# One expert's halves instead of two experts' quarters: how the second layer's expert weights are cut into transfers

## The chip, the cores and the metric

The kernel runs on one core of one Trainium2 chip. Its metric is the device time of one execution in microseconds (us); the median of three runs is used. A profile is one execution seen by the hardware profiler: which instruction ran when on which engine, what it waited for, and what the core's 16 transfer (DMA) engines moved.

## The reference

Two small networks run one after the other over 256 tokens of width 1024 (272 with the meta tokens of the first one). The part that matters is the mixture of experts in the first network, which comes twice, once per layer. Each token is sent to two of 32 experts, and each expert is three matrices:

```
def expert_block(args):
    xb, e = args
    hb = jax.nn.silu(xb @ w_gate[e]) * (xb @ w_up[e])
    return hb @ w_down[e]
```

`w_gate[e]` and `w_up[e]` are 1024 x 512, `w_down[e]` is 512 x 1024, all in 32-bit floats: 2 MB each, 6 MB an expert, 192 MB a layer. All 32 experts are read in both layers, since nearly every one has some tokens. Behind the second layer's experts come a layer norm and the second network (a state-space mixer, an MLP, attention, an MLP).

## The kernel before, in words

**Quads.** `moe(layer, ...)` works on four experts at a time, a quad; `qd` runs from 0 to 7, and its experts begin at `e0 = 4 * qd`. Each expert has 32 places for tokens. Four experts' 32 columns stand side by side on TensorE, so each matmul of line 983 (gate and up, 32 columns of stationary operand, 512 of moving weights) runs beside those of three other experts. A quad has 64 such products, which the trace shows as 128 matmul records (two for each), and 32 down products of line 1035, 64 records. Between them stand silu and the product hh (lines 1002 and 1003), four transposes of hh (line 1008), two of the token placement (1016) and a small gate product (1019). After the down products come eight records of line 1047, which carry the result back to the tokens. For every second quad, `gather` (line 935) brings the tokens of the next eight experts to their places.

**Weights.** `load(e)` fetches the 24 MB of a quad in 24 transfers of 1 MB, all issued on SP's queue by `fetch` (line 458), in program order. Each goes to the next buffer of a ring. There are two ways of cutting:

- `half(w, hf)`: one expert's half matrix a transfer, four transfers for the quad; every partition gets one run of 8 KB.
- `quarter(w, kq)`: a quarter matrix of two experts a transfer, two transfers for the quad; every partition gets two runs of 4 KB.

Gate and up products walk the pieces in the order in which they were fetched. With halves, 16 products (32 records) use four buffers, and the loop over the four experts is the innermost one; with quarters, 8 products (16 records) use two. A down half serves 16 products (32 records), a down quarter 8 (16 records). The choice is made on lines 910 to 916:

```
fine = layer == 1 and e >= FINE
if fine:
    gu = [[quarter(I[nm], kq) for nm in ("moe_w_gate", "moe_w_up")] for kq in range(4)]
else:
    gu = [[half(I[nm], hf) for nm in ("moe_w_gate", "moe_w_up")] for hf in range(2)]
if e < 28:
    return gu, [quarter(I["moe_w_down"], j) for j in range(4)] if fine else [half(I["moe_w_down"], hf) for hf in range(2)]
```

With FINE = 8, quads 0 and 1 of the second layer come in halves, as all of the first layer does; quads 2 to 7 come in quarters. The last quad's down matrices (e = 28) are cut by columns, in both kernels alike (lines 918 to 922).

**Buffers.** The ring has 17 buffers of 1 MB when the second layer's experts begin. The generator `stages()` is advanced at seven places in each quad (lines 986, 1005, 1027, 1056, 1060); after 14 steps, within quad 2 and after its loads have been placed, it gives up all but six buffers and adds two (`self.shrink(); self.grow(2)`). So quads 3 to 7 have eight. The space goes to `s5_prepare`, the preparation of the state-space mixer, which the following steps of the same generator put between the experts' instructions (lines 1258 to 1504): DVE computes small tables (W on lines 1405 to 1409, CL on 1424 to 1428), and TensorE turns them (lines 1371, 1373, 1415, 1437, 1458). A transfer into a buffer waits on SP until the matmuls that read the buffer's previous contents are done; all later transfers stand behind it on that queue.

**Order.** Each engine works through its instructions in one fixed order, which is set when the program is built; independent instructions of later steps can be put ahead of waiting ones in it. This is how gathers and the preparation come to stand between gate, up and down products.

Of the kernel before, what the change touches and what calls it, by code (L numbers as in the profile page):

```python
# [40 lines left out]
KV = 1  # L41
WARMB = 3
G3 = 5
FINE = 8
EARLY = 1, 0
N0 = 3
FAST = (0, 1), (0, 1)
# [26 lines left out]
class Net:  # L74
# [709 lines left out]
    def moe(self, layer, rows, stages=()):  # L784
# [10 lines left out]
        with ExitStack() as ph:  # L795
# [94 lines left out]
            def load(e):  # L890
# [18 lines left out]

                fine = layer == 1 and e >= FINE  # L910
                if fine:
# [1152 lines left out]
```

## Time and profile before

| what | value |
|---|---|
| runs | 1826.03, 1827.01, 1830.57 us; median 1827.01 us |
| profiled execution: its time, its span | 1828.64 us, 1826.8 us |
| TensorE (PE) busy | 1555.8 us (85%) |
| VectorE (DVE) busy | 851.4 us (47%) |
| ScalarE (ACT) busy | 504.8 us (28%) |
| SP's transfer queue | 532.04 MB, 76.9% of 16 engines' span |
| experts, first layer | from 142 us (first gate product) to 595 us (last down product) |
| experts, second layer | from 719 us to 1197 us, likewise |

The span runs from the first to the last instruction; the execution's own time is 1.8 us more. Busy shares are averages over stages with different limits. In the experts' stages the transfer engines are nearly always busy, and what the queue moves in a GB/s figure is the measure of progress; in the stages behind them TensorE is. A row of the timeline merges neighbouring instructions of one line, and what stands in square brackets is the idle time before it and what ended that.

### The profile page before, as it was taken

Reading aid. Unit: us, or ns where it says so; the run is one execution under the profiler, and the core shown is the slowest. Engines: PE = TensorE matmul, PEld = TensorE weight load, DVE = VectorE, ACT = ScalarE, POOL = GpSimd, SP = SyncE. Lnnn points to the kernel's source line nnn. Section 1 sums busy time; section 2 is a strip of 40 time slices with the busy share of each in tenths; the row PEclk is TensorE's granted clock in tenths of the full one; section 3 lists DMA queues with packets and bytes.
Section 4 is the critical chain, followed back from the end, with each engine's and each line's share of the span. In section 5 each row is a group of like instructions: output and inputs, shape, how many; then the busy total and the mean of one; then the engine's idle time right before and its main releaser. Section 6 shows DMA issues by size and latency. Waiting matters only on the chain.

```text
span 1826.8 us, 24952 instructions
## 1 busy us (share of the span) xinstructions
PE 1555.8 (85%) x10068; PEld 1022.4 (56%) x10076; DVE 851.4 (47%) x1812; ACT 504.8 (28%) x813; POOL 122.4 (7%) x185
## 2 busy tenths in 40 slices
PE   7898777877886899787696797678999999999997
PEld 6773322311322897232152252157989998889997
DVE  5962111201311874111552265069676556975655
ACT  4721000100000542110110110034454444655441
POOL 3000000000100321000000010012100000100100
PEclk9988989988999999998898898899999999999999
DMA  9449999999999866999999999994745542445520
GB/s 303 158 185 380 420 420 420 420 419 420 410 420 390 322 239 234 420 415 401 395 388 407 368 376 409 389 210 166 251 141 183 190 148 101 162 154 183 187 100 24
DMA packets 150522, 535.59 MB, mean 293 GB/s; under 512 B 23141, under 2 KB 35686, under 8 KB 120698
## 3 DMA queue, kind: packets, MB, share of 16 engines
q1 hardware_dynamic: 148226, 532.04, 76.9%
q0 software_dynamic: 1856, 1.75, 0.4%
q8 instruction: 82, 1.34, 0.3%
q14 instruction: 46, 0.38, 0.1%
q10 hardware_dynamic: 312, 0.07, 0.0%
HBM read 526.49 MB, written 1.05 MB: 289 GB/s over the span
## 4 chain that ended last, share of the span: by engine, by line
PE 36%; DMA 14%; DVE 7%; ACT 2%; issue 1%; SPq 1%; POOL 1%; DVEq 0%; ACTq 0%; POOLq 0%
DMA raw<-in_moe_w_up 7%; PE mm L502 5%; PE mm L504 5%; PE mm L503 5%; DMA raw<-in_moe_w_down 4%; PE tp L503 3%; PE tp L502 3%; PE tp L504 3%; PE mm L983 3%; DMA raw<-in_moe_w_gate 3%; PE mm L1035 2%; PE tp L935 1%; PE tp L1458 1%; SPq L96 1%; DVE raw L1575 1%
## 5 line engine op out<-in xcount | busy, mean ns | idle before, releaser
L983 PE MATMUL mm<-raw,xg 128*32 128x512 f32 x2048 | 371.9, 690 | 144.3 <-DMA raw<-in_moe_w_up 86.7
L295 DVE TENSOR_TENSOR wlo<-raw,whi 128x1024 fp32r<-128x1024 f32 (+3 forms) x265 | 280.3, 1073 | 162.6 <-ACT whi L294 161.8
L983 PEld LDWEIGHTS mm<-raw,xg 128*32 128x32 f32 x2048 | 82.2, 121 | 408.0 <-DMA raw<-in_moe_w_up 151.4
L294 ACT CAST whi<-raw 128x1024 fp32r<-128x1024 f32 (+3 forms) x265 | 238.9, 920 | 243.8 <-PE mm L504 101.5
L1003 DVE TENSOR_TENSOR hh<-hh,mm 128x512 f32<-128x512 f32 x16 | 11.0, 688 | 416.0 <-PE mm L983 391.3
L1035 PE MATMUL mm<-raw,ht 128*32 128x512 f32 (+2 forms) x1120 | 191.5, 593 | 13.8 <-DMA raw<-in_moe_w_down 13.2
L502 PE MATMUL mm<-whi,f 128*128 128x512 f32 (+3 forms) x432 | 149.9, 347 | 0.0
L503 PE MATMUL mm<-wlo,f 128*128 128x512 f32 (+3 forms) x432 | 149.8, 347 | 0.0
L504 PE MATMUL mm<-whi,f 128*128 128x512 f32 (+3 forms) x432 | 149.2, 345 | 0.2 <-DVE f L419 0.2
L503 PE MATMUL tp<-f,whi 128*128 128x256 f32 x512 | 146.0, 285 | 2.6 <-DVE f L419 2.5
L502 PE MATMUL tp<-f,whi 128*128 128x256 f32 x512 | 145.5, 285 | 0.4 <-ACT f L413 0.4
L504 PE MATMUL tp<-f,wlo 128*128 128x256 f32 x512 | 145.6, 284 | 0.0
L1035 PEld LDWEIGHTS mm<-raw,ht 128*32 128x32 f32 x1120 | 48.1, 114 | 119.5 <-issue 83.4
L1002 ACT ACTIVATE hh<-mm 128x512 f32<-128x512 f32 x16 | 9.6, 597 | 359.2 <-PE mm L983 359.2
L503 PEld LDWEIGHTS tp<-f,whi 128*128 128x128 f32 x512 | 99.0, 193 | 3.2 <-DVE f L419 3.2
L502 PEld LDWEIGHTS tp<-f,whi 128*128 128x128 f32 x512 | 98.7, 193 | 1.3 <-ACT f L413 0.9
L504 PEld LDWEIGHTS tp<-f,wlo 128*128 128x128 f32 x512 | 99.1, 194 | 0.0
L503 PE MATMUL mm<-xl,whi 128*128 128x272 f32 (+2 forms) x320 | 93.1, 292 | 0.7 <-DVE xl L295 0.4
L502 PE MATMUL mm<-xh,whi 128*128 128x272 f32 (+2 forms) x320 | 92.3, 292 | 0.9 <-ACT xh L422 0.5
L504 PE MATMUL mm<-xh,wlo 128*128 128x272 f32 (+2 forms) x320 | 91.7, 289 | 0.0
L502 PEld LDWEIGHTS mm<-whi,f 128*128 128x128 f32 x432 | 81.8, 189 | 10.3
L504 PEld LDWEIGHTS mm<-whi,f 128*128 128x128 f32 x432 | 81.5, 189 | 10.4 <-DVE f L419 0.5
(617 smaller groups left out, 2378.2 us busy)
## 6 DMA issues: line engine op xcount, KB each, us to landing
raw<-in_moe_w_gate SPq DMA_DIRECT2D x128, 1024.0 KB, 14.3
raw<-in_moe_w_up SPq DMA_DIRECT2D x128, 1024.0 KB, 19.9
raw<-in_moe_w_down SPq DMA_DIRECT2D x120, 1024.0 KB, 18.0
raw<-in_w_ff SPq DMA_DIRECT2D x64, 1024.0 KB, 5.1
raw<-in_sc_w_in SPq DMA_DIRECT2D x12, 1024.0 KB, 12.4
raw<-in_lru_w_in SPq DMA_DIRECT2D x8, 1024.0 KB, 13.7
raw<-in_ssm_w_glu SPq DMA_DIRECT2D x8, 1024.0 KB, 10.5
raw<-in_moe_w_down SPq DMA_DIRECT2D x12, 512.0 KB, 13.3
```

Of the source, the lines that this page charges most:

```text
L96: return lambda *a, **k: self.tc.keep_in_program_order(f(*a, **k))
L294: f(self.nc.scalar.copy)(hi, src)
L295: f(self.nc.vector.tensor_tensor)(lo, src, hi.bitcast(F32), op=OP.subtract)
L502: mm(out, lhsT=lh, rhs=rh, start=first, stop=False, skip_group_check=shared)
L503: mm(out, lhsT=lh, rhs=rl, start=False, stop=False, skip_group_check=shared)
L504: mm(out, lhsT=ll, rhs=rh, start=False, stop=last, skip_group_check=shared)
L935: nc.tensor.matmul(o, lhsT=hk[n][:, k, :], rhs=P[n], start=n == 0, stop=n == 1)
L983: nc.tensor.matmul(gu[m][i * 32:(i + 1) * 32, :], lhsT=xg[hf][:, k, c], rhs=wgu[hf * n + part][m][i][:, k % (4 // n), :], start=hf == 0 an ...
L1003: v.tensor_tensor(hh, hh, gu[1], op=OP.mult)
L1035: nc.tensor.matmul(o[e * 32:(e + 1) * 32, :], lhsT=ht[:, j, e * 32:(e + 1) * 32], rhs=w[e], start=j == 0, stop=j == 3)
L1458: nc.tensor.matmul(po[:, e, j:4, :], lhsT=sel[:, 67 - 64 * g - j:195 - 64 * g - j], rhs=t[:, g, :, 0:4 - j, :], start=e == slice(0, 8) and ...
L1575: v.tensor_tensor(o[:, :, 1:64], m2[:, :, 0:63], t[:, :, 0:63], op=OP.mult)
```

## The change

One constant: the first expert of the second layer whose quad comes in quarters. With 32 there is none, so `half` serves all quads of both layers, apart from the last quad's down matrices, which stay cut by columns.

```
@@ -41,7 +41,7 @@
 KV = 1
 WARMB = 3
 G3 = 5
-FINE = 8
+FINE = 32
 EARLY = 1, 0
 N0 = 3
 FAST = (0, 1), (0, 1)
```

The order in which the queue fetches a quad changes with it: gate and up alternate in groups of four transfers instead of two, and the down matrices come as two groups of four instead of four groups of two. The number of transfers, their size, and the number of matmuls stay the same.

## Rows read from the trace of the kernel before

**Rows 1.** Windows: stretch, length, busy PE, PEld, DVE, ACT, POOL, PEclk, DMA share, GB/s.
```profile
200.00:260.00 60.00, 47.43 (x244) 18.96 (x236) 10.27 (x22) 4.82 (x8) 0.00 (x0) 0.96 1.01 420
...
900.00:920.00 20.00, 13.58 (x94) 4.82 (x96) 2.40 (x8) 2.26 (x4) 0.00 (x0) 1.00 1.02 409
940.00:960.00 20.00, 20.00 (x144) 11.75 (x144) 7.67 (x12) 3.46 (x5) 0.00 (x0) 1.00 0.98 376
...
1005.00:1025.00 20.00, 17.75 (x108) 6.86 (x108) 8.67 (x16) 4.07 (x7) 0.00 (x0) 0.89 0.86 315
1080.00:1100.00 20.00, 20.00 (x145) 10.82 (x139) 16.19 (x40) 2.76 (x4) 5.75 (x6) 1.00 0.92 335
...
866.00:1168.00 302.00, 232.03 (x1450) 99.68 (x1449) 131.00 (x318) 33.81 (x55) 10.37 (x16) 0.90 1.00 392
```

**Rows 2.** Waits, 850 (DVE: 866) to 1170: us in total, times, longest.
```profile
SPq L458 <- PE mm L983: 113.1, 53, 8.9
SPq L458 <- PE mm L1035: 92.2, 24, 11.2
...
PE tp L1415 <- DVE W L1409: 14.7, 3, 6.9
...
PE mm L1035 <- DMA raw<-in_moe_w_down: 0.6, 1, 0.6
...
DVE hh L1003 <- PE mm L983: 61.9, 3, 25.4
```

**Rows 3.** The page, DMA packets of the whole span by size.
```profile
DMA packets 150522, 535.59 MB, mean 293 GB/s; under 512 B 23141, under 2 KB 35686, under 8 KB 120698
```

**Rows 4.** Timeline of TensorE, quad 3 into quad 4: start us, length us, what.
```profile
911.13 1.91 PE L983 MATMUL mm<-raw,xg 128*32 128x512 f32 x12 [1.51 <-DMA raw<-in_moe_w_up]
913.90 0.75 PE L1008 MATMUL tp<-ident,hh 128*128 128x128 f32 x4 [0.86 <-DVE hh L1003]
...
928.87 1.94 PE L1035 MATMUL mm<-raw,ht 128*32 128x512 f32 x16
...
942.54 1.91 PE L1035 MATMUL mm<-raw,ht 128*32 128x512 f32 x8
...
955.50 6.95 PE L983 MATMUL mm<-raw,xg 128*32 128x512 f32 x57
```

**Rows 5.** Timeline of TensorE, quad 4 into quad 5.
```profile
979.94 0.74 PE L1008 MATMUL tp<-ident,hh 128*128 128x128 f32 x4 [0.86 <-DVE hh L1003]
...
994.88 3.63 PE L1035 MATMUL mm<-raw,ht 128*32 128x512 f32 x24
...
1011.96 1.91 PE L1035 MATMUL mm<-raw,ht 128*32 128x512 f32 x8
...
1016.46 7.07 PE L983 MATMUL mm<-raw,xg 128*32 128x512 f32 x64
```

**Rows 6.** Timeline of TensorE, quad 6 into quad 7.
```profile
1117.98 1.13 PE L1008 MATMUL tp<-ident,hh 128*128 128x128 f32 x4 [6.23 <-DVE hh L1003]
...
1128.65 1.91 PE L1035 MATMUL mm<-raw,ht 128*32 128x512 f32 x8 [0.60 <-DMA raw<-in_moe_w_down]
...
1138.89 4.06 PE L983 MATMUL mm<-raw,xg 128*32 128x512 f32 x16 [1.42 <-DMA raw<-in_moe_w_up]
```

**Rows 7.** Timelines of SP and TensorE: a gate quarter's issue, and its first matmul.
```profile
1018.41 1.16 SPq L458 DMA_DIRECT2D raw<-in_moe_w_gate  x2
...
1023.71 1.05 PE L983 MATMUL mm<-raw,xg 128*32 128x512 f32 x4 [0.17 <-DMA raw<-in_moe_w_gate]
```

**Rows 8.** Timeline of TensorE, quad 5 into quad 6.
```profile
1044.40 0.74 PE L1008 MATMUL tp<-ident,hh 128*128 128x128 f32 x4 [0.86 <-DVE hh L1003]
...
1048.57 6.67 PE L1035 MATMUL mm<-raw,ht 128*32 128x512 f32 x32
...
1071.29 1.91 PE L1035 MATMUL mm<-raw,ht 128*32 128x512 f32 x8
...
1086.70 1.91 PE L983 MATMUL mm<-raw,xg 128*32 128x512 f32 x12
```

More of the change, by code (lines that the diff above doesn't have):

```diff
@@ L43 @@
 G3 = 5
-FINE = 8
+FINE = 32
 EARLY = 1, 0
```

## Prediction, made before the changed kernel was built or run

> **What bounds the kernel now.** I read the page first, then the stage of the second layer's experts by windows, then what the transfer queue and the engines wait for there, and last TensorE's order of work at the four places where one quad (four experts) hands over to the next.
>
> The windows give the two rates of a full transfer queue [rows 1]. With 8 KB runs (first layer, 200 to 260 us) it moves 420 GB/s, so a MB takes 1.048576/0.420 = 2.50 us. With 4 KB runs (900 to 920 us) it moves 409 GB/s, 2.56 us. Quads 3 to 7 of the second layer, 866 to 1168 us, average 392 GB/s: the bytes moved at 409 would take 302 x 392/409 = 289.5 us, so 12.5 us are lost. Three windows hold most of that: 376, 315 and 335 GB/s in 20 us each lose 1.6 + 4.6 + 3.6 = 9.8 us. The other 2.7 us are spread out, and I leave them as they are.
>
> The waits say whose those gaps are [rows 2]. The queue waits 113.1 us for the gate and up matmuls (L983) and 92.2 us for the down matmuls (L1035) to give a buffer back. Most is harmless, because megabytes issued earlier are still moving; the three slow windows are where they ran out. Down matmuls wait 0.6 us for data in the whole stretch: their weights are there long before TensorE comes to them. So the stage is bound by transfers as long as TensorE gives buffers back in time, and at the end of a quad it is late.
>
> **The change, part by part.** Quads 2 to 7 keep 24 transfers of 1 MB each; no instruction is added or dropped on TensorE, and SP issues as many. What moves is (1) the run length, (2) the order of bytes, and (3) how many buffers one stretch of matmuls holds.
>
> (1) Runs. 136 MB (quads 2 to 6, and gate and up of quad 7) go from 4 to 8 KB runs: 136 x (2.564 - 2.497) = 9.1 us less when the queue is full, of which quad 2 has 24 x 0.067 = 1.6. That long runs reach the engines uncut can be counted: the page has 150,522 - 120,698 = 29,824 packets of 8 KB [rows 3], and the 232 MB that already come in halves make 232 x 128 = 29,696. The Trainium skill ("DMA: Bandwidth & Descriptors", section on why small descriptors are slow) charges about 3 cycles a packet beside one per 32 bytes: 131 cycles for 4 KB against 129.5 a half of 8 KB, 1.2%. By that rule the gain is an estimated 4 us, and the sum below would end 5 us higher; the rows show 2.7%, and I take the rows.
>
> (2) and (3) Buffers. From quad 3 on there are eight. A quarter's 16 matmuls hold two and give them back together; six remain ahead. A half's 32 matmuls go through four experts in the inner loop, so all four buffers come back only with the last 8 of the 32. The groups of a quad are now gate-1, up-1, gate-2, up-2, down-1, down-2, four MB each, and each goes into the buffers of the group but one before it. So next quad's gate-1 waits for down-1 to be read, its up-1 for down-2, its gate-2 for its own gate-1.
>
> Call T the arrival of up-2's last MB, S the start of the four transposes of hh (L1008). Now S comes 2.8 us after T (911.13, 913.90) [rows 4]. With halves 26 matmuls instead of 12 are left at T. A row of 64 takes 7.07 us, 0.11 each [rows 5], so 14 more cost 1.5 us: S = T + 4.3, rounded to 4.5 because some stretches run slower (16 take 4.06 us at 1138.89 [rows 6]). On a queue that has run dry, issue to use takes 5.3 us (issue 1018.41, matmul 1023.71) [rows 7]. On a full queue down-2 ends at T + 20 and the next MB at T + 22.5. Let a, b and c be the times from S to the end of the 32nd down matmul, the 64th, and next quad's 32nd gate matmul. Then the queue stands idle, where the value is above zero,
> - ahead of gate-1 for a + 4.5 + 5.3 - 22.5 = a - 12.7,
> - ahead of up-1 for b - g - 10, with g the larger of a and 12.7 (four MB take 10 us),
> - ahead of gate-2 for c - u - 10, with u the larger of b and g + 10.
>
> I take a, b and c from before's rows, since there TensorE works through these stretches with next to no wait for data:
> - Quad 3 [rows 4]: S 913.90; the 32nd is the eighth of the 16 at 928.87, about 929.9; the 64th ends 944.45; the 32nd gate matmul is the ninth of the 57 at 955.50, about 957. a = 16.0, b = 30.6, c = 43.1. Idle 3.3 + 4.6 + 2.5 = 10.4 us.
> - Quad 4 [rows 5]: S 979.94; the eighth of 24 at 994.88, about 996; 1013.87; half of the 64 at 1016.46, about 1020.1. a = 16.0, b = 33.9, c = 40.2. Idle 3.3 + 7.9 + 0 = 11.2 us.
> - Quad 5 [rows 8]: S 1044.40; 1055.24; 1073.20; 1088.61. a = 10.8, b = 28.8, c = 44.2. Idle 0 + 6.1 + 5.4 = 11.5 us.
> - Quad 6 [rows 6]: S 1117.98, b = 1130.56 - 1117.98 = 12.6, c under 25. No idle.
>
> Together 33.1 us. a and b are this long because the program puts the state-space preparation and the next quads' gathers between the down matmuls: 64 of these alone take some 13 us (32 in 6.67 [rows 8]). A wait inside gate and up can cost too: TensorE waits for DVE's W three times, 14.7 us in all, 6.9 at most [rows 2]; the one in quad 3 falls into up-1's reading and now delays up-2. Reading a group takes 3.5 us and a restart 5.3 - 2.5 = 2.8, which leaves 3.7 of the 10 us of the next group, so this costs between 0 and 3 us; I take 1, as part of the wait falls where TensorE has no weights yet. SP stays behind a waiting issue for the same time as the idle sum; only weights are queued there, and nobody else waits on SP in this stage.
>
> Sum for quads 3 to 7: bytes at the long-run rate 302 x 392/420 = 281.9, spread loss 2.7, idle 34.1: 318.7 us against 302, **+16.7**. Quad 2, on the seventeen buffers, -1.6. The last quad's down columns keep their form and follow up-2 as before: 0. After the experts every phase starts from their result, so the rest only shifts. +15.1 on the profiled execution's 1828.6 is 1843.7; that execution is 1.6 over the median, so **1842**.
>
> Bounds. The waits for DVE inside b and c might not move along: if W is ready at the same absolute time, most of its 14.7 us drop out of them; with 11 gone, +4 is left: 1831. If TensorE works at the slower spacing of [rows 6] at each up-2, 3 us more in four quads, or if W comes later too (below), +12 to +15: 1857.
>
> **Rivals.**
> - *Only the rate counts, faster.* The order on TensorE is made when the program is built, and other waits may draw the side work out of the down stretches into gate and up, where TensorE idles. Should a stay under 12.7, b under 22.7 and c under 32.7 in each quad, no new gap opens, and 281.9 + 12.5 = 294.4 us: with quad 2, -9.2, 1818. For it: quad 6 already looks so. Against: three of four quads don't, and the side work has to go somewhere; TensorE is busy for 232 of the 302 us [rows 1]. The Trainium skill ("Trainium Kernel Development and Optimization", best practices) says to double-buffer so that transfers overlap with compute. Four buffers read while four fill is just that, and by that rule alone this rival would hold. The trace speaks against it: with groups of two, and so six MB ahead instead of four, the queue already falls to 315 GB/s.
> - *The two cancel.* If the waits for W stay where they are and half of the side work moves, idle is about 20 us instead of 34: 1828, within the measurement.
> - *DVE is late too, slower still.* hh on DVE waits 61.9 us for gate and up [rows 2], and DVE works in order: what it prepares for TensorE stands behind hh. As hh comes later in each quad, W does too, and the 14.7 us double: 1857. Against it: DVE is busy 131 of 302 us [rows 1] and can catch up.
> - *It doesn't do what it says*: runs might be cut anyway. The packet count [rows 3] excludes this for the first layer's form, which is the same code.
>
> **How the numbers follow.** A measurement tells about 0.3%, 5.5 us, from no change. The forecast's case, starving by fours, has 0.66; DVE late too 0.14; cancelling 0.08; the rate alone 0.12. So faster 0.12, same 0.08, slower 0.80. The range from 1826 to 1862 leaves out the rate alone and the far end of the case in which DVE is late too.
>
> **What would show it.** Right: windows without idle at 420 GB/s, between 870 and 1190 us gaps of 3 to 8 us at three of the quad boundaries, issues of gate-1 right after the 32nd down matmul, and the stage of experts about 15 us longer with everything after it shifted alike. More packets of 8 KB by 136 x 128 = 17,408. Wrong: a mean in the stage above 400 GB/s, down matmuls packed closely with no side work between them, or full windows still at 409.

## The result, and the profile after

The changed kernel takes 1853.83 us (median of four runs, 1850.14 to 1857.42) against 1828.55 (1826.03 to 1830.57) in the runs of the kernel before beside them: ratio 1.0128, interval 1.0111 to 1.0146, so it is slower by 20 to 27 us, 23.4 by the ratio. The prediction said slower, by 15.1 us, to 1842 (set on 1827.01, the median of the three runs shown ahead of it). The direction, the range and the mechanism held; the size was too small.

First, where the time lies. The stage of the second layer's experts, from its first gate product to the start of its last down row, lasts 1196.10 - 719.48 = 476.6 us before and 1220.02 - 722.33 = 497.7 after: 21.1 of the 24.0 us between the two profiled executions (1852.63 and 1828.64). Another 2.9 lie ahead of the stage, where both kernels issue the same instructions. They belong to that execution: in a second profile of the changed kernel (the run *changed again* below) the stage starts at 719.65 and lasts 500.6 us, 24.0 more than before. The last down row of the kernel before:

```profile
1196.10 1.06 PE L1035 MATMUL mm<-raw,ht 128*32 128x128 f32 x26 [1.44 <-DMA raw<-in_moe_w_down]
```

The windows of the changed kernel: first the three slow ones of [rows 1] and the whole stretch of quads 3 to 7, then stretches cut at the handovers from quad to quad (stretch, length, busy PE, PEld, DVE, ACT, POOL, granted clock, DMA share, GB/s):

```profile
940.00:960.00 20.00, 19.17 (x106) 11.34 (x102) 8.73 (x15) 3.75 (x6) 0.00 (x0) 1.00 0.71 280
...
1005.00:1025.00 20.00, 12.27 (x54) 4.81 (x49) 13.83 (x27) 4.30 (x7) 0.00 (x0) 0.83 0.62 238
1080.00:1100.00 20.00, 19.23 (x106) 11.39 (x105) 8.24 (x14) 4.13 (x6) 0.96 (x2) 1.00 0.64 255
...
866.00:1168.00 302.00, 235.97 (x1390) 101.22 (x1388) 133.54 (x333) 33.67 (x54) 9.57 (x16) 0.90 0.90 362
...
925.00:975.00 50.00, 44.91 (x319) 25.32 (x318) 22.19 (x37) 8.31 (x13) 0.98 (x2) 0.99 0.80 313
975.00:995.00 20.00, 15.55 (x84) 5.70 (x82) 1.64 (x6) 1.18 (x2) 0.00 (x0) 0.84 1.01 422
995.00:1040.00 45.00, 33.41 (x180) 13.38 (x181) 17.75 (x32) 6.05 (x10) 0.00 (x0) 0.85 0.84 339
1040.00:1065.00 25.00, 15.53 (x143) 5.79 (x142) 1.64 (x6) 1.26 (x3) 0.97 (x2) 1.00 1.01 420
1065.00:1125.00 60.00, 53.97 (x314) 27.11 (x308) 35.83 (x75) 8.60 (x13) 5.72 (x8) 0.94 0.77 306
```

The same three handovers in the kernel before:

```profile
925.00:975.00 50.00, 42.58 (x282) 21.56 (x280) 20.58 (x35) 6.20 (x9) 0.00 (x0) 0.97 1.01 388
...
995.00:1040.00 45.00, 30.66 (x180) 9.50 (x178) 17.84 (x32) 5.30 (x9) 0.00 (x0) 0.89 0.95 367
...
1065.00:1125.00 60.00, 49.61 (x311) 25.49 (x311) 40.17 (x98) 7.03 (x11) 6.71 (x8) 0.91 0.99 384
```

Between the handovers the long runs do move 420 GB/s. In the handovers the queue falls to 313, 339 and 306. A window's loss is its length times the share missing from the full rate: after, at 420, 12.7 + 8.7 + 16.3 = 37.7 us; before, at 409, 2.6 + 4.6 + 3.7 = 10.9. That is +26.8. The windows 850 to 925 and 1125 to 1170 lose 3.2 more than before (401 GB/s from 850 to 900, 388 from 900 to 925 and 407 from 1145 to 1170; before 396, 408 and 407). With the run length's -9.1 the sum is +20.9, and the stage measures 21.1.

The page of the changed kernel, packets by size:

```profile
DMA packets 133115, 535.59 MB, mean 289 GB/s; under 512 B 23142, under 2 KB 35687, under 8 KB 85883
```

133,115 - 85,883 = 47,232 packets of 8 KB; before there were 29,824 [rows 3]. The difference is the predicted 17,408.

Waits of the changed kernel, 850 (DVE: 866) to 1170 us: total, times, longest, to be set beside [rows 2]:

```profile
SPq L458 <- PE mm L983: 147.1, 27, 14.4
SPq L458 <- PE mm L1035: 108.4, 14, 19.2
...
PE tp L1415 <- DVE W L1409: 14.9, 3, 7.1
PE tp L1008 <- DVE hh L1003: 6.6, 5, 3.2
...
DVE hh L1003 <- PE mm L983: 77.2, 3, 33.1
```

The transfer queue waits half as often as before, each time longer (27 waits for gate and up instead of 53, longest 14.4 instead of 8.9). The waits for W are as they were.

SP's timeline of the changed kernel shows what the queue waits for: the groups of four, start and length in us, that are issued late (the groups in between are left out).

```profile
935.48 2.06 SPq L458 DMA_DIRECT2D raw<-in_moe_w_gate  x4
952.12 2.21 SPq L458 DMA_DIRECT2D raw<-in_moe_w_up  x4
964.25 2.19 SPq L458 DMA_DIRECT2D raw<-in_moe_w_gate  x4
...
1005.63 2.19 SPq L458 DMA_DIRECT2D raw<-in_moe_w_gate  x4
1022.73 2.06 SPq L458 DMA_DIRECT2D raw<-in_moe_w_up  x4
1030.24 2.09 SPq L458 DMA_DIRECT2D raw<-in_moe_w_gate  x4
...
1069.70 1.75 SPq L458 DMA_DIRECT2D raw<-in_moe_w_gate  x4
1090.64 2.12 SPq L458 DMA_DIRECT2D raw<-in_moe_w_up  x4
1107.12 2.00 SPq L458 DMA_DIRECT2D raw<-in_moe_w_gate  x4
1119.11 2.00 SPq L458 DMA_DIRECT2D raw<-in_moe_w_up  x4
```

TensorE's timeline of the changed kernel in the same stretches, and its last down row:

```profile
913.32 6.59 PE L983 MATMUL mm<-raw,xg 128*32 128x512 f32 x26 [1.45 <-DMA raw<-in_moe_w_up]
...
920.77 0.75 PE L1008 MATMUL tp<-ident,hh 128*128 128x128 f32 x4 [0.85 <-DVE hh L1003]
...
932.67 3.62 PE L1035 MATMUL mm<-raw,ht 128*32 128x512 f32 x20
...
969.47 1.04 PE L983 MATMUL mm<-raw,xg 128*32 128x512 f32 x2 [1.13 <-DMA raw<-in_moe_w_gate]
...
976.95 6.02 PE L983 MATMUL mm<-raw,xg 128*32 128x512 f32 x30 [0.58 <-DMA raw<-in_moe_w_gate]
...
986.92 3.62 PE L983 MATMUL mm<-raw,xg 128*32 128x512 f32 x26 [1.45 <-DMA raw<-in_moe_w_up]
991.39 0.75 PE L1008 MATMUL tp<-ident,hh 128*128 128x128 f32 x4 [0.85 <-DVE hh L1003]
...
1056.93 3.62 PE L983 MATMUL mm<-raw,xg 128*32 128x512 f32 x26 [1.45 <-DMA raw<-in_moe_w_up]
...
1061.40 0.74 PE L1008 MATMUL tp<-ident,hh 128*128 128x128 f32 x4 [0.85 <-DVE hh L1003]
...
1112.18 1.04 PE L983 MATMUL mm<-raw,xg 128*32 128x512 f32 x2
...
1116.30 7.05 PE L983 MATMUL mm<-raw,xg 128*32 128x512 f32 x58
...
1220.02 1.91 PE L1035 MATMUL mm<-raw,ht 128*32 128x128 f32 x26 [1.51 <-DMA raw<-in_moe_w_down]
```

Read the two together at quad 4's start. The row of down records at 932.67 holds the last of the first 32, and within it, at 935.48, SP issues four gate transfers at once: they had waited for just that. The next four come 16.6 us later, with the end of the second 32, though four MB take only 10 us: 6.6 us of an idle queue. At 964.25 gate-2 follows when the new quad's gate-1 has been read, again 12.1 us later. Its first matmul stands at 969.47, 5.2 us behind the issue, the restart of [rows 7]. The same three steps begin at 1005.63 and at 1069.70, though not every one of them leaves the queue idle there (see the sums by quad below).

### The profile page after: what moved, and what is told of

Read it like the earlier page. It is cut to its first block, busy times and chain, and to the rows that moved or that the text cites. A ratio compares the mean times of both kernels' runs of the same rounds, so it can differ in the third digit from the quotient of the medians.

```text
span 1850.9 us, 24958 instructions
## 1 busy us (share of the span) xinstructions
PE 1575.6 (85%) x10075; PEld 1028.7 (56%) x10076; DVE 851.7 (46%) x1812; ACT 505.1 (27%) x813; POOL 122.5 (7%) x185
## 2 busy tenths in 40 slices
DMA packets 133115, 535.59 MB, mean 289 GB/s; under 512 B 23142, under 2 KB 35687, under 8 KB 85883
## 4 chain that ended last, share of the span: by engine, by line
PE 36%; DMA 14%; DVE 6%; ACT 2%; SPq 1%; issue 1%; POOL 0%; DVEq 0%; ACTq 0%; POOLq 0%
DMA raw<-in_moe_w_up 10%; PE mm L502 5%; PE mm L503 5%; PE mm L504 5%; DMA raw<-in_moe_w_down 4%; PE tp L503 3%; PE mm L983 3%; PE tp L502 3%; PE tp L504 3%; PE mm L1035 2%; PE tp L935 1%; PE tp L1458 1%; SPq L96 1%; DVE raw L1575 1%; PE mm L105 1%
## 5 line engine op out<-in xcount | busy, mean ns | idle before, releaser
L983 PE MATMUL mm<-raw,xg 128*32 128x512 f32 x2048 | 382.9, 687 | 152.2 <-DMA raw<-in_moe_w_up 91.9
L983 PEld LDWEIGHTS mm<-raw,xg 128*32 128x32 f32 x2048 | 86.2, 123 | 423.9 <-DMA raw<-in_moe_w_up 160.0
L1035 PE MATMUL mm<-raw,ht 128*32 128x512 f32 (+2 forms) x1120 | 200.0, 579 | 17.6 <-DMA raw<-in_moe_w_down 16.8
L504 PEld LDWEIGHTS mm<-whi,f 128*128 128x128 f32 x432 | 81.5, 189 | 10.4 <-DVE f L419 0.5
## 6 DMA issues: line engine op xcount, KB each, us to landing
raw<-in_ssm_w_glu SPq DMA_DIRECT2D x8, 1024.0 KB, 10.4
raw<-in_moe_w_down SPq DMA_DIRECT2D x12, 512.0 KB, 13.3
```

What stands on the lines that cost most here:

```text
L504: mm(out, lhsT=ll, rhs=rh, start=False, stop=last, skip_group_check=shared)
L983: nc.tensor.matmul(gu[m][i * 32:(i + 1) * 32, :], lhsT=xg[hf][:, k, c], rhs=wgu[hf * n + part][m][i][:, k % (4 // n), :], start=hf == 0 an ...
L1035: nc.tensor.matmul(o[e * 32:(e + 1) * 32, :], lhsT=ht[:, j, e * 32:(e + 1) * 32], rhs=w[e], start=j == 0, stop=j == 3)
```

## The experiments

The theory: a group of four that comes back as one leaves too little ahead of the queue at a handover, and the side work (state-space preparation, gathers) between the down matmuls makes the handover long. Against it stood: the form of the halves costs something itself; buffers alone don't matter; a late DVE does it.

**Depth: seventeen buffers.** The ring keeps its 17 buffers, and the preparation comes only behind the experts, so both causes are gone; first with halves (changed kernel), then with quarters (kernel before), by the same edit. These two kernels and the next two ran once each; what counts are their windows.

```
-NY = 14
+NY = 48
```

> Halves in all quads, but the ring keeps its 17 buffers up to the last quad: the state-space preparation, which wants their space, comes behind the seventh quad instead of between quads 2 and 6. Total time is not the point (the preparation then stands uncovered at the end); the windows are. Starving of eight buffers held by fours (the forecast): with 13 MB ahead of a group that is being read, no handover runs dry, and 880 to 1100 us move 417 to 421 GB/s. Rival, a cost of halves themselves (more matmuls left after the last arrival, four buffers given back at once, vectors later): the windows stay well under 417, near the 362 to 366 of the changed kernel where the rival is all of it.

> The same with quarters from quad 2 on. It measures the run length by itself, with buffers to spare: 880 to 1100 us at 407 to 410 GB/s, so 0.067 us a MB, and the stretch of 96 MB in quads 3 to 6 some 6.4 us longer than with halves. If run length were not the cause of the two rates, both kernels would show the same GB/s.

Halves, window 880 to 1100, and SP's waits from 850 to 1100 us:

```profile
880.00:1100.00 220.00, 165.67 (x830) 56.61 (x827) 30.42 (x58) 13.36 (x22) 9.97 (x16) 0.93 1.01 419
```
```profile
SPq L458 <- PE mm L983: 3.4, 11, 0.4
```

Quarters, the same window:

```profile
880.00:1100.00 220.00, 156.78 (x806) 50.19 (x806) 30.34 (x57) 13.14 (x22) 10.11 (x16) 0.97 1.03 408
```

Nothing starves. With halves the queue waits 3.4 us in 250 for gate and up matmuls; with quarters it waits 62.1 for them, but with megabytes under way, since the rate stays full. So the halves' form costs nothing by itself here, and the rate of the long runs is real: 419 against 408 GB/s, 2.7%. By the rule of the Trainium skill that the prediction weighed ("DMA: Bandwidth & Descriptors", why small descriptors are slow) it would be 1.2%; the measurement decides. Both kernels are much longer in all (1939.25 and 1943.64 us), because the preparation is left without cover behind the experts: DVE's busy time in the window is 30 us, where the changed kernel has 83, and with halves the DMA engines move 1 GB/s from 1200 to 1250 us and nothing from 1250 to 1300, where the preparation now stands.

**Side work: eight buffers without it.** The ring shrinks as ever, but the preparation waits for the end; again in the changed kernel and in the kernel before.

```
-N0 = 3
+N0 = 33
```

> Halves on eight buffers as in the changed kernel, but with the state-space preparation behind the seventh quad; the gathers stay where they are. The forecast says that a handover runs dry only because side work stands between the down matmuls: without it a and b shrink to about 7 and 13 us, or 12 to 16 and 22 where a gather of 9 us stands there, so idle is 0 to 3 us a handover and 880 to 1100 us move 405 to 418 GB/s. Rival, eight buffers held by fours starve by themselves: under 385 GB/s.

> Quarters on eight buffers, with the preparation behind the seventh quad. If its work between the matmuls is what empties the queue, no window between 880 and 1100 us is under 405 GB/s, also where a gather stands, since six MB are ahead: 407 to 410 in the whole stretch. If eight buffers are too few even so: gaps at the gathers as with halves (365 and 383 GB/s in 40 us).

Halves, then quarters, 880 to 1100 us:

```profile
880.00:1100.00 220.00, 167.61 (x794) 53.62 (x798) 28.78 (x52) 12.79 (x21) 6.15 (x8) 0.88 0.98 404
```
```profile
880.00:1100.00 220.00, 162.14 (x803) 49.69 (x803) 29.57 (x53) 12.57 (x21) 6.04 (x8) 0.95 1.03 409
```

The changed kernel moves 360 GB/s in this window and the kernel before 389. Without the preparation the quarters have no gap left. The halves keep two: 404 GB/s, a little under what was expected. What is missing lies in 900 to 940 (365 GB/s) and 1020 to 1060 (383), 8.8 us together, where the gathers for the next quads still stand among the down matmuls; in the other 40 us pieces it is 420 or 421. The changed kernel loses 220 x (1 - 360/420) = 31.4 us in this window. So eight buffers are enough for either form where no side work stretches the handover; the gathers alone already empty the queue with halves, and not with quarters. In all they take 1935.96 and 1931.17 us, for the same reason as above.

**Depth alone: quarters with six buffers.** In groups of two, four MB stay ahead, as with halves in eight buffers.

```
         self.shrink()
-        self.grow(2)
```

> The kernel before with six buffers instead of eight from quad 3 on. A group of two then has 4 MB ahead, as a group of four has on eight buffers. If depth ahead is what counts (the forecast), re-timing before's matmuls on six buffers gives +19 us (+13 to +28) over before, nearly what halves cost, with gaps at the same handovers. If halves cost by their own form, quarters on six buffers stay within +8 us of before.

```profile
880.00:1100.00 220.00, 165.69 (x1090) 74.59 (x1082) 84.94 (x174) 27.27 (x43) 2.92 (x6) 0.92 0.94 364
```

1851.51 us, ratio 1.0109 (1.0057 to 1.0162), 20 us slower than before, with neither the runs nor the order of bytes touched. So most of the change's cost in time can be had without halves, by taking two MB of depth away. That the totals agree this well is in part chance, for the losses lie differently. In the three handover windows this kernel moves 347, 337 and 355 GB/s and loses 23.4 us at its full rate of 409, where the changed kernel loses 37.7 at 420 and the kernel before 10.9; another 5.3 us go at 850 to 900 (366 GB/s), where the changed kernel loses 2.3. With the same four MB ahead, groups of four cost the handovers 26.8 us and groups of two 12.5: what is left ahead is not the whole of it; the size of the group, or the order of bytes that comes with it, counts too, and these two weren't separated. More than eight buffers beside the preparation weren't tried, for want of space.

**One part of the change alone.** Halves for gate and up only (changed kernel, down by quarters again), and halves for down only (kernel before).

```
-return gu, [quarter(I["moe_w_down"], j) for j in range(4)] if fine else [...]
+return gu, [quarter(I["moe_w_down"], j) for j in range(4)] if layer == 1 and e >= 8 else [...]

-return gu, [quarter(I["moe_w_down"], j) for j in range(4)] if fine else [...]
+return gu, [quarter(I["moe_w_down"], j) for j in range(4)] if False else [...]
```

> Gate and up in halves, down in quarters from quad 2 on. The forecast charges three waits at a handover: gate-1 for the first down half, up-1 for the second, gate-2 for gate-1. Down quarters give two buffers back after 16 matmuls, which feeds gate-1 and up-1 earlier; gate-2 and the wait within gate and up stay. Re-timing before's matmuls this way: +19 us over before (+12 to +24). If the down halves were nearly all of the cost: under +8.

> Gate and up in quarters from quad 2 on, down in halves. Gate and up follow each other by twos, but the first four MB of the next quad wait for 32 down matmuls at a time. Re-timing: +8 to +13 us over before. Under +4 if only gate and up starve; +20 or more if the down halves are the whole cost.

Gate and up: 1844.57 us, ratio 1.0084 (1.0061 to 1.0106), +15.4, as expected. Down: 1848.21, 1.0100 (1.0078 to 1.0122), +18.3, where 8 to 13 was expected. Together they would be 33.7, but the whole change costs 23.4. A likely reason, not shown, is that the parts share their waits, since a queue that is held up by one group has less to wait for at the next. Part of the surplus in the second has a mark of its own on TensorE, in quad 6:

```profile
1140.42 1.13 PE L1008 MATMUL tp<-ident,hh 128*128 128x128 f32 x4 [11.73 <-DVE hh L1003]
```

Before, the wait at this place was 6.23 us [rows 6], and in the changed kernel it is 3.2. Here DVE is late with hh; the down matrices behind it are read late, and 1145 to 1170 moves 343 GB/s, some 4 us lost. So the rival "DVE is late too" exists as a mechanism, in this kernel and not in the changed one.

**Run length alone.** Changed kernel, each half of quads 2 to 7 by two transfers with 4 KB runs into the same buffer, twice; the second time beside the changed kernel itself.

```
-out.append(self.fetch(src[:, hf * k:hf * k + k, :], [128, k, src.shape[2]]))
+if layer == 1 and e >= 8:
+    t = self.fetch(None, [128, k, src.shape[2]])
+    for r in (slice(0, k // 2), slice(k // 2, k)):
+        nc.sync.dma_start(t[:, r, :], src[:, hf * k:hf * k + k, :][:, r, :])
+    out.append(t)
+else:
+    out.append(self.fetch(src[:, hf * k:hf * k + k, :], [128, k, src.shape[2]]))
```

> The changed kernel, but each 1 MB half of quads 2 to 7 is fetched by two transfers of 0.5 MB with runs of 4 KB; buffers, order and matmuls stay. It takes the rate gain away and leaves the starving. 136 x 0.067 = 9.1 us at most; where the queue is idle for TensorE part of it is hidden, so +4 to +9 us over the changed kernel, +25 to +34 over before. If the longer runs gave nothing here: equal to the changed kernel within 3 us. Twice the issues on SP could add a little by themselves.

> The changed kernel once more, beside the next one. 1.0128 of before was measured; the prediction's sum says 1.008, and the profiled execution stood 2.85 us late before the second layer's experts even began. Between 1.011 and 1.014 if the two profiles' difference (some 22 us from there on) is the whole of it.

> Halves with 4 KB runs, on the same chip and beside the same runs as the changed kernel. If the long runs' 9.1 us reach the end, this is 9 us slower than the changed kernel. If the queue, where it is faster, only meets TensorE earlier and waits longer (three handover stretches lost 32 us at 409 GB/s with short runs, 38 us at 420 with long ones), 2 to 5 us of them are left. If nothing is left: equal within 2 us.

With 4 KB runs: 1851.96 us, ratio 1.0128 (1.0104 to 1.0152), and 1853.61, 1.0130 (1.0113 to 1.0147). The changed kernel again: 1852.86, 1.0130 (1.0113 to 1.0147). Beside each other they are 0.75 us apart, which four runs of each tell to some 3 us; 4 to 9 were expected at first, and the 9.1 us of the long runs can't be seen at the end. The stage lasts 498.6 and 502.1 us with 4 KB runs, 497.7 and 500.6 without: 1.2 us on average. SP's timeline of the second 4 KB run (each half is two issues) and one row of its TensorE show where the rest is:

```profile
963.23 4.03 SPq L900 DMA_DIRECT2D raw<-in_moe_w_gate  x8
...
1028.45 6.89 SPq L900 DMA_DIRECT2D raw<-in_moe_w_gate  x8
...
1105.54 4.20 SPq L900 DMA_DIRECT2D raw<-in_moe_w_gate  x8
```
```profile
975.48 6.17 PE L989 MATMUL mm<-raw,xg 128*32 128x512 f32 x30 [0.64 <-DMA raw<-in_moe_w_gate]
```

From one gate-2 to the next are 65.2 and 77.1 us here, and 66.0 and 76.9 in the changed kernel (964.25, 1030.24, 1107.12; its second profile has 66.1 and 77.0). Two quads of 24 MB would differ by 48 x 0.067 = 3.2 us if the rate counted, the long runs being the shorter; they are 0.6 longer. So a quad that waits for TensorE at its handover is, here, about as long as TensorE makes it. The three handover windows lose 35.6 us at 409, the changed kernel beside it 41.4 at 420: 5.8 of the 9.1 us are waited instead of moved. The edit halves the transfers too, and small pieces are in use sooner: the fourth expert's gate half 12.25 us behind the issue here (975.48 - 963.23), 12.70 in the changed kernel (976.95 - 964.25), though four MB last 0.27 longer. So a part of the balance, some 0.7 us a restart, may be the pieces' and not the waits'. 4 KB runs in pieces of 1 MB, in the order of the halves, weren't tried.

**Halves where nothing starves.** Kernel before, quarters in quads 3 to 6 only, so that quads 2 and 7 get long runs.

```
-fine = layer == 1 and e >= FINE
+fine = layer == 1 and e in (12, 16, 20, 24)
```

> Quarters in quads 3 to 6 alone; quad 2, which still has 17 buffers, and gate and up of quad 7, ahead of which hardly any side work stands, come in halves. 40 MB at the higher rate: -2.7 us against before if neither starves (the forecast), so 0.9985 of before. If quad 7 starves by fours: +2 to +5.

```profile
866.00:1168.00 302.00, 234.60 (x1472) 100.39 (x1474) 131.39 (x322) 34.01 (x55) 10.55 (x16) 0.91 1.01 396
```

1827.13 us over twelve runs, ratio 0.9992 (0.9979 to 1.0005): 1.5 us less, with an interval from 3.8 less to 0.9 more. The 2.7 expected lie in it, and so does nothing. Quad 7 doesn't starve in halves (419 GB/s from 1125 to 1145 us and 411 from 1145 to 1170, before 409 and 407), so the harm comes from quads 3 to 6.

**Seventeen buffers for longer.** Kernel before, the shrink moved seven steps later, quarters in quads 4 to 6 only.

```
-NY = 14
+NY = 21
-fine = layer == 1 and e >= FINE
+fine = layer == 1 and e in (16, 20, 24)
```

> A version to beat both: the ring keeps 17 buffers for one more quad (0 to 3), all of which come in halves, quarters only in quads 4 to 6, and the preparation starts a quad later, so that its end falls into quad 7, where DVE and TensorE have little to do. Gain: 24 + 24 + 16 MB at the higher rate 4.3 us, and the handover from quad 3 to 4 no longer starves (2 to 3 us): -5 to -7 us against before. Against it: what is left of the preparation after quad 7 stands uncovered, 0 to 15 us.

1845.88 us, ratio 1.0075 (1.0052 to 1.0097): +14, where a gain of 5 to 7 was expected. From 866 to 1000 us the queue now moves 402 GB/s, but the preparation is packed into fewer quads: 995 to 1040 falls to 348 and 1065 to 1125 to 368, and what is left of it delays the last down rows, which wait for DVE:

```profile
1215.32 1.94 PE L1035 MATMUL mm<-raw,ht 128*32 128x128 f32 x32 [7.45 <-DVE y L1039]
```

Before, the last of these rows started at 1196.10. The side work has to lie somewhere, and where it now lies it costs more. No version here beats the kernel before by more than the measurement can tell.

## Why the prediction was right and where it failed

**Right: the mechanism.** Groups of four hold the queue at the handovers with side work, and the size of the group against the depth of the ring decides. The seventeen-buffer, six-buffer and no-side-work kernels each show one side of it; the six-buffer kernel also shows that depth is not all, since groups of two with the same four MB ahead add less than half as much idle time to the handovers.

**Right: the small steps.** Packets of 8 KB: 17,408 more. Restart 5.3 us: 5.2. S behind T 4.5 us: 991.39 - 986.92 and 1061.40 - 1056.93 are 4.47 each. Quad 6 hands over without a gap worth the name (407 GB/s from 1145 to 1170 us).

**The idle sum by quad.** With the predicted bookkeeping on the issue times above (a queue that ran dry restarts 5.3 us behind the issue, a full one would go on at T + 22.5, four MB take 10):

- Quad 3: predicted 10.4, now 5.0 + 6.6 + 2.1 = 13.7 (window 12.7). The last up records took 6.59 us at 913.32, where 26 take 3.62 at 986.92, so S came 7.45 us behind T. From 913.3 to 919.9 us the mean granted clock is 0.54, close to the lower of the two levels (1.2 GHz), where 986 to 991 has 1.00, the upper (2.4 GHz). Ahead of it TensorE had waited three times, some 1.5 us each, for an expert's up weights. The prediction's upper bound had this case, 3 us a quad; in the first profile it came in one quad of three. It goes with the 1.7 us ahead of gate-1. The other 2.0 stand ahead of up-1: the second 32 down matmuls end 16.6 us behind the first, where b - a = 14.6 was taken.
- Quad 4: predicted 11.2, now 1.5 + 7.1 + 0 = 8.6 (window 8.7).
- Quad 5: predicted 11.5, now 0 + 6.5 + 6.5 + 2.0 = 15.0 (window 16.3). The 2.0 stand ahead of *up-2*: 1119.11 - 1107.12 is 12.0, and four MB take 10. In the second profile of the changed kernel it is 15.2, so 5.2, and in both profiles with 4 KB runs it is 15.2 as well.

The second profile of the changed kernel, quad 6's gate-2 and up-2, two rows of quad 3 on TensorE, and the last handover window:

```profile
1104.94 2.11 SPq L458 DMA_DIRECT2D raw<-in_moe_w_gate  x4
1120.13 1.97 SPq L458 DMA_DIRECT2D raw<-in_moe_w_up  x4
```
```profile
910.85 5.08 PE L983 MATMUL mm<-raw,xg 128*32 128x512 f32 x26 [1.45 <-DMA raw<-in_moe_w_up]
...
924.18 3.53 PE L1035 MATMUL mm<-raw,ht 128*32 128x512 f32 x4
```
```profile
1065.00:1125.00 60.00, 54.53 (x309) 28.05 (x301) 37.30 (x87) 8.04 (x12) 6.83 (x8) 0.89 0.71 283
```

60 x (1 - 283/420) = 19.6 us, 3.3 more than in the first. In quad 3 the slow stretch costs the same here, some 3 us, but split over the two rows (5.08 us where 3.62 would do, 3.53 where four such records took 1.90 at 928.13 in the first profile).

The idle sum of the handovers by wait, over quads 3 to 5, with the same bookkeeping on both profiles' issue times (us):

| idle ahead of | predicted | first profile | second profile |
|---|---|---|---|
| gate-1 | 6.6 | 6.5 | 6.6 |
| up-1 | 18.6 | 20.2 | 20.7 |
| gate-2 | 7.9 | 8.6 | 8.6 |
| up-2 | none | 2.0 | 5.2 |
| together | 33.1 | 37.3 | 41.1 |

**The step that failed** is the list of idle times: "ahead of gate-1", "ahead of up-1", "ahead of gate-2", and no more. Up-2 waits for the quad's own up-1, and in quad 6 that is read late, since gathers and preparation also stand between the gate and up records themselves (single pairs at 1112.18 and before it, the closed row only from 1116.30). The missing wait is 2.0 of the 4.2 us by which the list was short in the first profile, and 5.2 of 8.0 in the second; most of the rest is up-1, which was read 2.0 too short in quad 3. That gate-1 came out is luck: 1.7 too little in quad 3 and 1.8 too much in quad 4.

The text saw a late up-2 at one place, in quad 3 itself, and took 1 us. There it measures 2.0 (252 GB/s from 900 to 905 us) and 2.2 in the second profile (238 from 895 to 900).

By the windows the handovers cost 37.7 and, in the second profile, 41.4 us where 33.1 was summed. Outside them "2.7 spread out, I leave them as they are" and that 1 us were too little: the changed kernel loses 3.2 us more there than before, 1.7 in the second profile. Before's own loss in these handovers is 10.9, not 9.8. Together 15.1 + 4.6 + 2.2 - 1.1 = 20.8 (stage: 21.1) and 15.1 + 8.3 + 0.7 - 1.1 = 23.0 (stage: 24.0).

**The run length** had its rate right and its worth wrong. A reader of the sum would take it that 9.1 us are saved. With 4 KB runs the stage would have been 6.0 us longer by the sum's own thresholds (12.7 becomes 13.3, and 10 becomes 10.26, which gives 3.1 of the 9.1 back in idle time). It measured 1.2. How much of the difference is owed to the smaller pieces stays open.

**The rivals.** "Only the rate counts": a, b and c stayed long (14.7, 31.4 and 43.5 us in quad 3, by the issues above), excluded. "The two cancel": the waits for W stayed, but so did the side work, and the handovers lose 37.7 us, not 20; excluded. "DVE is late too": TensorE waits 14.9 us for W against 14.7, and 6.6 for hh against 9.7 (the row below is the kernel before, 850 to 1170 us); it isn't the cause here. "It doesn't do what it says": the packets say it does.

```profile
PE tp L1008 <- DVE hh L1003: 9.7, 5, 6.2
```

## What to carry to other kernels

In a ring of buffers like this one, count not the buffers but what is left ahead of the queue while the largest group that comes back as one is being read, and set that against the longest stretch between two such returns, side work included; a larger group makes that stretch longer. Follow each group of the cycle to its own wait, the ones in the middle too. A faster transfer is worth its rate only for the bytes that move between the last wait and the result that TensorE needs next; where the queue waits for buffers anyway, it mostly waits longer.

## What was not expected

- 2.7% in rate (419 against 408 GB/s over 220 us) left 0.75 us, known to some 3 us, in the median of an execution with 136 MB of such runs.
- Halves for gate and up alone cost 15.4 us, for down alone 18.3, both together 23.4.
- The same instructions on the same data differ by up to 3.3 us ahead of the stage: its first gate product starts between 719.35 and 722.63 us in the fourteen profiles of this case.
